# First token group: down projection of nine pairs in seven products of eight, and the sums of w_down made there

## The chip, the cores and the metric

The kernel runs on one core of one Trainium2 chip. Its engines, by the names that the profile gives them, are PE (TensorE; PEld is its weight load), DVE (VectorE), ACT (ScalarE), POOL (GpSimd) and SP (SyncE, which here only issues transfers). The metric is the device time of one execution in microseconds; the runs shown are compared by their median. The profile is of one further execution, whose times are counted from its first instruction.

## The reference

One layer of a hybrid decoder is computed for 2048 prompt tokens and 8 single decode tokens, 2056 columns in all, in float32. What the change touches is the feed-forward part behind the mixing of tokens:

```python
hn = _rmsnorm(h, norm2_g)
ff = jax.nn.silu(jnp.einsum('btd,df->btf', hn, w_gate)) * jnp.einsum('btd,df->btf', hn, w_up)
y = h + jnp.einsum('btf,fd->btd', ff, w_down)
```

The model width is 1024 and the width of `ff` 2816. A last normalisation of `y` gives the output.

## The kernel before

Values are transposed: features lie on the 128 partitions, tokens along the row. A float32 operand is held as a high part (a cast to fp32r, made by ACT) and a low part (value minus high part, a subtraction on DVE or POOL), and a product is three matmuls: high by high, high by low, low by high.

The program has two phases. The first (norm, input projection, recurrence, attention, output projection) takes the first 679 us. The second is the feed-forward part. It runs over three token groups (`HALVES`), each of two halves of 344 or 342 tokens. Within a group it runs over 11 pairs of 128-wide chunks of `ff` (`NPAIR`). In each pair the gate and the up projection are 2 × 2 block products done in seven products instead of eight (Strassen-Winograd; `PRODS` is their order), 12 matmuls each. Their weight blocks are partly sums of blocks: group 0 makes these on POOL (`mixed_weights`, L1259), splits all seven blocks of gate and up (L1224 and L1225, engines by `E_LO0`) and stores four of them split; groups 1 and 2 load those four and split only the other three (`E_LO1`, `E_LO2`).

`products` then makes the activations: ACT and DVE bring the results out of PSUM (L1410, L1431 to L1438), silu is on ACT (L1389), the multiply on POOL or DVE (L1392). The helper `part` casts a block on ACT (L1380) and subtracts on DVE (L1381).

The down projection has two forms, chosen by `wino(gi, p)`:

- plain: `down_weights` loads and splits four blocks of w_down per pair (POOL does all four subtractions), and `down` does 96 matmuls into 16 PSUM tiles `pd`, each followed by one add into `y` on DVE (L1469).
- in seven products: `down_make` loads quarters of w_down, forms eight half-wide sums (L1326, engines by `E_DSUM`), splits them in seven tiles `wd` (`split_parts`, L1293 and L1294) and stores five tiles of sums to `sums_d`; `down_load` reads the stored ones instead of forming them. `products` makes three more blocks of activations from four differences (L1399 to L1406, engines by `E_T1`, `E_T2`) and splits seven blocks instead of four. `down_parts` does 84 matmuls in 14 rounds, with 28 adds into `y` on DVE (L1500). Its rounds are spread between the products of the next pair.

Pairs 0 and 10 always use the plain form. Pairs 1 to 9 use the second form in groups 1 and 2, and the plain one in group 0. Group 1 runs `down_make`, group 2 `down_load`.

The order on each engine is fixed when the program is built. Each piece of work is a generator that yields the time for which it is planned; `plan()` lays these out from `wino` and a few constants (`U_M` for a product, `U_D` for a plain down projection, `U_R` for a round), and a scheduler turns the priorities into one list per engine. `PE_ORDER` writes the order on PE out by hand up to pair 1 of group 0. Weights go through 7 raw tiles and 8 split tiles in turn, sums of weights through 5 tiles (`sqp`, `bcp`), and larger blocks through 16 tiles of `bigp`.

Of the kernel before, what the change touches and what calls it, by code (L numbers as in the profile page):

```python
# [10 lines left out]
ALU = mybir.AluOpType  # L11
AX = mybir.AxisListType

P = 128
# [22 lines left out]
NPAIR = NF // 2  # L37
# [27 lines left out]
E_LO0 = ['V', 'V', 'V', 'V', 'P', 'P', 'P']  # L65
E_LO1 = ['P', 'V', 'P']
E_LO2 = ['V', 'V', 'P']
E_DLO1 = ['P', 'P', 'P', 'V', 'P', 'V', 'V']
E_DLO2 = ['V', 'P', 'V', 'P', 'V', 'V', 'P']
E_DSUM = ['P', 'P', 'P', 'P', 'P', 'P', 'P', 'V']  # L70
E_T1 = ['P', 'P', 'P', 'P']
E_T2 = ['P', 'V', 'P', 'P']
E_HN = ['P', 'V', 'P', 'P']
# [1 line left out]


def wino(gi, p):
    return gi > 0 and 0 < p < NPAIR - 1


def plan():
# [23 lines left out]
T_B, T_END, T_PROD, T_DOWN, T_ROUND = plan()  # L105
# [182 lines left out]
def hybrid_step(tc, xT, xR, vecs, cst, gatew, win, wout, wgate, wup, wdown, kT, vC, ck, cv, sconv, sh0,  # L288
                yT, pkT, pvT, pconv, phs, skw, svw, sconv_o, sh_o):
    nc = tc.nc  # L290
    ch = Chains(tc)
    at, ahead, fire = ch.at, ch.ahead, ch.fire
    with ExitStack() as ctx:
# [179 lines left out]
        def eng(x):  # L473
            return nc.gpsimd if x == "P" else nc.vector
# [703 lines left out]
        with ExitStack() as bctx:  # L1178
# [32 lines left out]
            def t_prod(gi, p, x, i):  # L1211
                return T_PROD[gi, p, x, i]
# [20 lines left out]
            def mixed_weights(src, gi, p, x):  # L1233
# [5 lines left out]
                if gi:  # L1239
                    for i, r in enumerate(PRODS):  # L1240
# [9 lines left out]
                        else:  # L1250
                            keep_weights((x, gi, p, r), f"{x}{gi}_{p}_{r}", v, eng((E_LO1, E_LO2)[gi - 1][(1, 2, 4).index(r)]))
                    return
# [38 lines left out]
            def split_parts(gi, p, j, v):  # L1291
                w = whl_tile(f"wd{gi}_{p}_{j}").rearrange("p a (b c) -> p a b c", b=2)
                nc.scalar.copy(w[:, :, 0], v)  # L1293
                eng((E_DLO1, E_DLO2)[gi - 1][j]).tensor_tensor(  # L1294
                    w[:, :, 1], v, w[:, :, 0].bitcast(F32), op=ALU.subtract)
                ws["d", gi, p, j] = w
                fire(("d", gi, p, j))
# [62 lines left out]
            def products(gi, p, x):  # L1360
                nn = HALVES[gi][0][1]
                name = f"{x}{gi}_{p}"
                up = x == "u"
                if up:
                    fh = {(h, n): fp.tile([P, TP], F32R, tag=f"fh{h}{n}", name=f"fh{gi}_{p}_{h}{n}")
                          for h in range(2) for n in range(2)}
                    fl = {(h, n): fp.tile([P, TP], F32R, tag=f"fl{h}{n}", name=f"fl{gi}_{p}_{h}{n}")
                          for h in range(2) for n in range(2)}
                C = {(h, n): (gpb if up else gpa).tile([P, TP], F32, tag="c", name=f"c_{name}_{h}{n}") for h in range(2) for n in range(2)}
                if not up:  # L1370
                    gss[gi, p] = C
                c11, c12, c21, c22 = (C[h, n][:, :nn] for h in range(2) for n in range(2))
                combine = up and wino(gi, p)
                if combine and gi not in extra:
                    place = slots(bigp, "big", f"t{gi}", F32R)
                    extra[gi] = [next(place) for _ in range(6)]

                def part(r, v, place):
                    hi, lo = (x[:, :nn] for x in place)
                    nc.scalar.copy(hi, v)  # L1380
                    nc.vector.tensor_tensor(lo, v, hi.bitcast(F32), ALU.subtract)  # L1381
                    ts[gi, p, r] = hi, lo
                    fire(("T", gi, p, r))

                def finished(h, n, src=None):
                    v = C[h, n][:, :nn]
                    src = v if src is None else src
                    if not up:
                        seen[f"act{gi}_{p}_{h}{n}"] = nc.scalar.activation(v, src, AF.Silu)  # L1389
                        return  # L1390
                    g = gss[gi, p][h, n][:, :nn]
                    (nc.vector if p == NPAIR - 1 or src is not v else eng(E_MUL[2 * h + n])).tensor_tensor(  # L1392
                        v, src, g, op=ALU.mult)
                    if not combine:
                        part((h, n), v, (fh[h, n], fl[h, n]))
                    elif (h, n) != (0, 1):
                        part({(0, 0): 1, (1, 0): 2, (1, 1): 3}[h, n], v, (fh[h, n], fl[h, n]))
                    if combine and (h, n) == (0, 1):
                        eng((E_T1, E_T2)[gi - 1][0]).tensor_tensor(c11, c12, c11, op=ALU.subtract)  # L1399
                        part(5, c11, (fh[0, 1], fl[0, 1]))  # L1400
                    elif combine and (h, n) == (1, 0):
                        eng((E_T1, E_T2)[gi - 1][1]).tensor_tensor(c12, c22, c12, op=ALU.subtract)
                        eng((E_T1, E_T2)[gi - 1][2]).tensor_tensor(c22, c22, c11, op=ALU.subtract)
                        part(6, c22, extra[gi][0:2])
                        part(7, c12, extra[gi][2:4])
                        eng((E_T1, E_T2)[gi - 1][3]).tensor_tensor(c21, c21, c22, op=ALU.subtract)  # L1406
                        part(4, c21, extra[gi][4:6])

                def add(o, a, b, op=ALU.add):
                    nc.vector.tensor_tensor(o, a, b, op)  # L1410

                banks = {}
                for i, r in enumerate(PRODS):
                    yield t_prod(gi, p, x, i), (x, gi, p, r), ("hn", gi, r)
                    key = BANK[r]
                    fresh = key not in banks
                    if fresh:
                        banks[key] = acc_tile(f"ps_{name}_{r}")[:, :nn]
                    ps = banks[key]
                    w = ws.pop((x, gi, p, r))  # L1420
                    for kk in range(4):
                        hi, lo = hn[gi, r, kk]
                        hi, lo = hi[:, :nn], lo[:, :nn]
                        wh, wl = w[:, 0, kk * P:kk * P + P], w[:, 1, kk * P:kk * P + P]
                        first = fresh and kk == 0
                        mm(f"{name}_{r}", ps, wh, hi, start=first, stop=False, skip_group_check=not fresh)
                        mm(f"{name}_{r}", ps, wh, lo, start=False, stop=False, skip_group_check=not fresh)
                        mm(f"{name}_{r}", ps, wl, hi, start=False, stop=kk == 3, skip_group_check=not fresh)
                    with ahead(F_LEAD[5]):
                        if r == 1:  # L1430
                            nc.scalar.copy(c21, ps)  # L1431
                        elif r == 2:
                            add(c11, c21, ps)
                            finished(0, 0)
                        elif r == 6:
                            seen[f"c{name}_6"] = nc.scalar.copy(c12, ps)  # L1436
                        elif r == 5:
                            nc.scalar.copy(c22, ps)  # L1438
                        elif r == 7:
                            add(c22, c22, ps)  # L1440
                            finished(1, 1)
                        elif r == 3:
                            add(c12, c12, ps)
                            finished(0, 1)
                        else:
                            finished(1, 0, ps)
                fire((x + "done", gi, p))
# [152 lines left out]
            for gi in range(len(HALVES)):  # L1600
                tb = T_B[gi]
                if gi:
                    ch.add(hn_mix(gi, stage, T_MIX[gi], F_MIX[2 * gi - 1]))
                    ch.add(hn_load(gi, PRODS[:3], slots(bigp, "big", f"hn{gi}_0", F32R), tb - F_HN[0], U_M))
                ch.add(hn_load(gi, PRODS[3:], slots(hnp, "hn", f"hn{gi}_1", F32R), tb - F_HN[1], U_M, None if gi else stage))
                ch.add(y_load(gi, tb + F_HN[2]))
                for i, n in enumerate((1, 0)):
                    te = T_END[gi]
                    ch.add(finish(gi, n, te + F_FIN[0] + F_FIN[1] * i, 1.0) if gi < 2 else finish_last(n))
                for p in range(NPAIR):  # L1610
                    ch.add(mixed_weights(wgate, gi, p, "g"))
                    ch.add(mixed_weights(wup, gi, p, "u"))
                    ch.add((down_load if gi == 2 else down_make)(gi, p) if wino(gi, p) else down_weights(gi, p, T_DOWN[gi, p]))
                    ch.add(products(gi, p, "g"))
                    ch.add(products(gi, p, "u"))
                    ch.add((down_parts if wino(gi, p) else down)(gi, p))
# [113 lines left out]
```

## Time and profile before

| what | value |
|---|---|
| three runs | 2061.11 to 2063.26 us, median 2062.06 us |
| span of the profiled execution | 2054.6 us (the time from its first to its last instruction; its own device time is not given beside it, the median is 7.5 us above the span) |
| granted TensorE clock, mean | 0.997 |
| group 0, 720 to 1105 us | PE busy 385.00 of 385 us |
| group 1, 1181 to 1563 us | PE busy 376.44 of 382 us |
| group 2, 1640 to 2000 us | PE busy 360.00 of 360 us |

Busy time of an engine is the time in which one of its instructions was running. Stretches are given by their start and end in us from the first instruction. A group of instructions is told by the line of the kernel, the engine, the operation and the tiles that it writes and reads; a tile has the name that the code gives it (`pw` and `pd` are PSUM tiles of the down projection, `wd` and `w_d` its split weights, `sd` its sums, `fl` and `t` low parts of activations).

### The profile page before, as it was taken

What the parts mean: (1) busy time and instruction counts of PE and PEld (TensorE: products, weight loads), DVE (VectorE), ACT (ScalarE), POOL (GpSimd) and SP (SyncE); (2) the same over time, 40 slices, a digit from 0 to 9 for tenths busy, and PEclk for the clock granted to TensorE, in tenths of its full rate; (3) what the DMA queues carried; (4) which work ended last, traced back from release to release, by engine and by line L of the source; (5) the groups of instructions that cost most, each with busy time, mean ns of one, the idle gap of its engine ahead of it and who ended that gap; (6) DMA issues with size and microseconds to landing.
All of it is one profiled execution on the core that took longest, in us unless ns stands there. A gap on an engine that the chain in (4) does not pass through costs nothing.

```text
span 2054.6 us, 34857 instructions
## 1 busy us (share of the span) xinstructions
PE 2015.9 (98%) x12319; PEld 1908.1 (93%) x12319; DVE 1459.9 (71%) x2694; ACT 944.6 (46%) x1960; POOL 906.5 (44%) x799
## 2 busy tenths in 40 slices
PE   9999999999999999999999999999999999999998
PEld 9988787878777899999999999999999999999998
DVE  6877886767985766666654667777768666777675
ACT  6764774553664543343334533333335433433343
POOL 5311342020122787567656645556457522322333
PEclk9999999999999999999999999999999999999999
DMA  9864584576688856666546677776677675566652
GB/s 329 293 213 143 188 275 159 175 233 210 208 261 280 314 200 223 205 210 207 207 172 210 229 260 258 227 229 221 222 253 265 211 251 189 183 197 196 197 179 96
DMA packets 208991, 450.98 MB, mean 219 GB/s; under 512 B 25232, under 2 KB 82720, under 8 KB 208800
## 3 DMA queue, kind: packets, MB, share of 16 engines
q1 hardware_dynamic: 205184, 445.73, 65.2%
q10 hardware_dynamic: 3632, 3.02, 0.4%
q8 instruction: 97, 1.59, 0.3%
q14 instruction: 78, 0.64, 0.1%
HBM read 335.89 MB, written 113.84 MB: 219 GB/s over the span
## 4 chain that ended last, share of the span: by engine, by line
PE 77%; DVE 9%; DMA 6%; ACT 3%; issue 2%; POOL 1%; SPq 0%; DVEq 0%; ACTq 0%; POOLq 0%
PE ps_u L396 19%; PE ps_g L396 19%; PE pw L396 11%; PE pd L396 10%; PE ip L396 10%; PE op L396 4%; DMA n<-hs 3%; DMA xs<-in_xT 1%; DMA m<-mixed 1%; PE o L396 1%; PE pt L401 1%; DVE sc L974 1%; DVE sc L963 1%; PE s L396 1%; DMA mixed<-n 1%
## 5 line engine op out<-in xcount | busy, mean ns | idle before, releaser
L396 PE MATMUL ps_g<-hn,w_g 128*128 128x342 f32 (+1 forms) x2772 | 489.4, 320 | 4.6 <-DVE c_u L1410 1.8
L396 PE MATMUL ps_u<-hn,w_u 128*128 128x342 f32 (+1 forms) x2772 | 479.9, 319 | 1.9 <-ACT c_u L1436 1.3
L396 PEld LDWEIGHTS ps_g<-hn,w_g 128*128 128x128 f32 x2772 | 445.1, 188 | 6.0 <-DVE c_u L1410 2.3
L396 PEld LDWEIGHTS ps_u<-hn,w_u 128*128 128x128 f32 x2772 | 444.2, 188 | 2.6 <-ACT c_u L1436 1.6
L396 PE MATMUL ip<-xn,w_in 128*128 128x512 f32 (+1 forms) x1680 | 353.4, 358 | 1.9 <-ACT xn L431 1.8
L396 PEld LDWEIGHTS ip<-xn,w_in 128*128 128x128 f32 x1680 | 270.1, 189 | 46.0 <-issue 3.8
L1500 DVE TENSOR_TENSOR y<-y,pw 128x342 f32<-128x342 f32 x504 | 238.7, 504 | 73.0 <-PE pw L396 72.2
L396 PE MATMUL pd<-fh,w_d 128*128 128x344 f32 (+1 forms) x960 | 239.4, 320 | 0.6 <-DVE y L1469 0.6
L396 PE MATMUL op<-mix,w_out 128*128 128x512 f32 (+1 forms) x960 | 203.4, 357 | 0.5 <-DVE rrec L763 0.3
L396 PEld LDWEIGHTS op<-mix,w_out 128*128 128x128 f32 x960 | 155.4, 188 | 29.3 <-issue 5.0
L1469 DVE TENSOR_TENSOR y<-y,pd 128x344 f32<-128x344 f32 (+1 forms) x240 | 117.9, 507 | 75.3 <-PE pd L396 70.7
L396 PEld LDWEIGHTS pd<-fh,w_d 128*128 128x128 f32 x960 | 168.3, 188 | 1.4 <-DVE y L1469 1.1
L396 PE MATMUL pw<-fh,wd 128*128 128x342 f32 x576 | 165.6, 319 | 1.2 <-DVE y L1500 1.2
L396 PE MATMUL pd<-fl,w_d 128*128 128x344 f32 (+1 forms) x480 | 153.4, 320 | 0.0
L1381 DVE TENSOR_TENSOR fl<-c_u,fh 128x342 fp32r<-128x342 f32 (+1 forms) x132 | 107.1, 815 | 48.3 <-ACT fh L1380 47.9
L1225 POOL TENSOR_TENSOR w_u<-ru,w_u 128x512 fp32r<-128x512 f32 x44 | 58.9, 1338 | 181.6 <-ACT w_u L1224 155.0
L1392 POOL TENSOR_TENSOR c_u<-c_u,c_g 128x342 f32<-128x342 f32 (+1 forms) x60 | 60.5, 1008 | 170.7 <-DVE c_u L1410 132.1
L1380 ACT CAST fh<-c_u 128x342 fp32r<-128x342 f32 (+1 forms) x132 | 63.0, 480 | 157.8 <-POOL c_u L1392 61.9
L396 PE MATMUL pw<-t,wd 128*128 128x342 f32 x648 | 126.7, 320 | 2.6 <-DVE t L1381 1.7
L1410 DVE TENSOR_TENSOR c_u<-c_u,ps_u 128x342 f32<-128x342 f32 (+1 forms) x99 | 50.2, 507 | 100.3 <-PE ps_u L396 100.1
L396 PEld LDWEIGHTS pw<-t,wd 128*128 128x128 f32 x648 | 106.0, 188 | 4.4 <-DVE t L1381 2.5
L396 PEld LDWEIGHTS pw<-fh,wd 128*128 128x128 f32 x576 | 105.3, 189 | 1.7 <-DVE y L1500 1.5
(316 smaller groups left out, 3507.4 us busy)
## 6 DMA issues: line engine op xcount, KB each, us to landing
w_g<-split_g SPq DMA_DIRECT2D x88, 512.0 KB, 4.2
w_u<-split_u SPq DMA_DIRECT2D x88, 512.0 KB, 4.9
w_in<-split_w SPq DMA_DIRECT2D x84, 512.0 KB, 3.5
rg<-in_wgate SPq DMA_DIRECT2D x110, 256.0 KB, 3.1
ru<-in_wup SPq DMA_DIRECT2D x110, 256.0 KB, 3.2
w_out<-split_w SPq DMA_DIRECT2D x48, 512.0 KB, 4.4
split_g<-w_g SPq DMA_DIRECT2D x44, 512.0 KB, 3.6
split_u<-w_u SPq DMA_DIRECT2D x44, 512.0 KB, 2.7
```

The source lines that it names most:

```text
L396: r = nc.tensor.matmul(*args, **kw)
L401: r = nc.tensor.transpose(*args)
L963: seen[f"sm{gb}_{kv}_{g}"] = nc.vector.tensor_tensor_reduce(sc[:, g, :kn], ps[:, gi * 256:gi * 256 + kn], mask[:, k0:k0 + kn], -SCALE, ns[ ...
L974: nc.vector.tensor_scalar(sc[:, g, :kn], sc[:, g, :kn], mx[:, 1, g:g + 1], None, ALU.mult)
L1225: lo_eng.tensor_tensor(w[:, 1, :], src, w[:, 0, :].bitcast(F32), op=ALU.subtract)
L1380: nc.scalar.copy(hi, v)
L1381: nc.vector.tensor_tensor(lo, v, hi.bitcast(F32), ALU.subtract)
L1392: (nc.vector if p == NPAIR - 1 or src is not v else eng(E_MUL[2 * h + n])).tensor_tensor(v, src, g, op=ALU.mult)
L1410: nc.vector.tensor_tensor(o, a, b, op)
L1469: r = nc.vector.tensor_tensor(ys[gi, n, m], ys[gi, n, m], ps, ALU.add)
L1500: nc.vector.tensor_tensor(v, v, ps, ALU.add)
```

## The change

`wino` no longer leaves group 0 out, so that pairs 1 to 9 of group 0 take the form in seven products; two lists name the engines of its new subtractions and differences. Group 0 now runs `down_make`, and groups 1 and 2 run `down_load`. `plan()` follows from `wino` by itself; no other constant changes.

```diff
+E_DLO0 = ['P', 'V', 'P', 'V', 'P', 'V', 'V']
...
+E_T0 = ['P', 'P', 'P', 'P']
...
 def wino(gi, p):
-    return gi > 0 and 0 < p < NPAIR - 1
+    return 0 < p < NPAIR - 1
...
-                eng((E_DLO1, E_DLO2)[gi - 1][j]).tensor_tensor(
+                eng((E_DLO0, E_DLO1, E_DLO2)[gi][j]).tensor_tensor(
                     w[:, :, 1], v, w[:, :, 0].bitcast(F32), op=ALU.subtract)
...
-                        eng((E_T1, E_T2)[gi - 1][0]).tensor_tensor(c11, c12, c11, op=ALU.subtract)
+                        eng((E_T0, E_T1, E_T2)[gi][0]).tensor_tensor(c11, c12, c11, op=ALU.subtract)
...
-                    ch.add((down_load if gi == 2 else down_make)(gi, p) if wino(gi, p) else down_weights(gi, p, T_DOWN[gi, p]))
+                    ch.add((down_load if gi else down_make)(gi, p) if wino(gi, p) else down_weights(gi, p, T_DOWN[gi, p]))
```

The three other differences of `products` (L1402, L1403, L1406) get their engine from `E_T0` in the same way. 'P' is POOL and 'V' is DVE.

More of the change, by code (lines that the diff above doesn't have):

```diff
@@ L1398, in finished @@
                     if combine and (h, n) == (0, 1):
-                        eng((E_T1, E_T2)[gi - 1][0]).tensor_tensor(c11, c12, c11, op=ALU.subtract)
+                        eng((E_T0, E_T1, E_T2)[gi][0]).tensor_tensor(c11, c12, c11, op=ALU.subtract)
                         part(5, c11, (fh[0, 1], fl[0, 1]))
                     elif combine and (h, n) == (1, 0):
-                        eng((E_T1, E_T2)[gi - 1][1]).tensor_tensor(c12, c22, c12, op=ALU.subtract)
-                        eng((E_T1, E_T2)[gi - 1][2]).tensor_tensor(c22, c22, c11, op=ALU.subtract)
+                        eng((E_T0, E_T1, E_T2)[gi][1]).tensor_tensor(c12, c22, c12, op=ALU.subtract)
+                        eng((E_T0, E_T1, E_T2)[gi][2]).tensor_tensor(c22, c22, c11, op=ALU.subtract)
                         part(6, c22, extra[gi][0:2])
                         part(7, c12, extra[gi][2:4])
-                        eng((E_T1, E_T2)[gi - 1][3]).tensor_tensor(c21, c21, c22, op=ALU.subtract)
+                        eng((E_T0, E_T1, E_T2)[gi][3]).tensor_tensor(c21, c21, c22, op=ALU.subtract)
                         part(4, c21, extra[gi][4:6])
```

## The prediction

> **What bounds the kernel now.** I read the head of the page first, then the busy time by stretch, then single engines inside one stretch of each token group.
>
> ```profile
> span 2054.6 us, 34857 instructions
> PE 2015.9 (98%) x12319; PEld 1908.1 (93%) x12319; DVE 1459.9 (71%) x2694; ACT 944.6 (46%) x1960; POOL 906.5 (44%) x799
> ```
>
> The median of the runs is 2062.06 us, so 7.5 us lie outside the span; I add changes of the span to the median. PE is the bound as an average. The table by stretch (length, then busy time of PE, PEld, DVE, ACT, POOL) asks whether that holds in each group: rows one to three are the middles of groups 0, 1 and 2, the fourth is the passage from group 1 to group 2, the fifth the fullest DVE stretch that I found.
>
> ```profile
> 720.00:1105.00 385.00, 385.00 (x2451) 385.00 (x2450) 245.79 (x368) 152.73 (x303) 258.97 (x194) 1.00 0.59 202
> 1181.00:1563.00 382.00, 376.44 (x2384) 373.45 (x2383) 281.83 (x496) 136.59 (x277) 210.15 (x191) 1.00 0.71 235
> 1640.00:2000.00 360.00, 360.00 (x2295) 360.00 (x2294) 254.77 (x473) 134.36 (x271) 104.60 (x89) 1.00 0.63 200
> 1582.00:1622.00 40.00, 39.43 (x248) 38.63 (x247) 28.02 (x43) 20.50 (x49) 27.11 (x26) 1.00 0.76 265
> 1542.00:1582.00 40.00, 40.00 (x256) 40.00 (x255) 33.33 (x57) 21.08 (x47) 25.09 (x23) 1.00 0.75 248
> ```
>
> Group 0, which the change touches, never starves PE: 385.00 of 385. Group 1, which already does what group 0 is now to do, loses 382 − 376.44 = 5.6 us; group 2, which loads the sums instead of making them, loses none. The granted clock is 1.00 in all of them. So group 0 gains exactly as long as PE stays the bound there, and the question is what DVE and POOL have left.
>
> **What PE saves.** The price of a matmul comes from back-to-back work in the order of time:
>
> ```profile
> 740.05 7.24 PE L396 MATMUL ps_u<-hn,w_u 128*128 128x344 f32 x45
> 747.14 2.06 PE L396 MATMUL ps_g<-hn,w_g 128*128 128x344 f32 x12
> ```
>
> (747.14 − 740.05) / 45 = 0.1576 us. A pair of group 0 is 14 products of 12 matmuls and 96 for the down projection: 264, or 41.6 us. Seven products of eight need 84: 252, or 39.7 us. Nine pairs save 108 matmuls, **17.0 us**, if nothing stalls.
>
> **What DVE and POOL pay.** These are groups by line and shape, group 0 (720 to 1098 us) for what goes, group 1 (1222 to 1542 us) for what comes; busy us and mean ns stand behind the bar.
>
> ```profile
> L1469 DVE TENSOR_TENSOR y<-y,pd 128x344 f32<-128x344 f32 x145 | 72.1, 508 | 50.9 <-PE pd L396 50.6
> L1381 DVE TENSOR_TENSOR fl<-c_u,fh 128x344 fp32r<-128x344 f32 x36 | 26.5, 737 | 15.5 <-ACT fh L1380 15.5
> L1225 POOL TENSOR_TENSOR w_d<-rd,w_d 128x512 fp32r<-128x512 f32 x36 | 52.6, 1467 | 5.9 <-ACT w_d L1224 5.9
> L1500 DVE TENSOR_TENSOR y<-y,pw 128x342 f32<-128x342 f32 x222 | 103.4, 504 | 19.4 <-PE pw L396 19.1
> L1381 DVE TENSOR_TENSOR fl<-c_u,fh 128x342 fp32r<-128x342 f32 x30 | 28.1, 941 | 6.2 <-ACT fh L1380 5.9
> L1381 DVE TENSOR_TENSOR t<-c_u,t 128x342 fp32r<-128x342 f32 x24 | 21.1, 899 | 0.0
> L1294 DVE TENSOR_TENSOR wd<-rd,wd 128x512 fp32r<-128x512 f32 x16 | 16.0, 1003 | 0.0
> L1326 DVE TENSOR_TENSOR sd<-rd,rd 128x256 f32<-128x256 f32 x8 | 6.1, 767 | 7.3 <-DMA rd<-in_wdown 7.3
> L1294 POOL TENSOR_TENSOR wd<-rd,wd 128x512 fp32r<-128x512 f32 x16 | 22.3, 1395 | 16.4 <-ACT wd L1293 14.7 <-DVE c_u L1392 1.7
> L1326 POOL TENSOR_TENSOR sd<-rd,sd 128x256 f32<-128x256 f32 x15 | 14.8, 984 | 0.6
> L1326 POOL TENSOR_TENSOR rd<-rd 128x256 f32<-128x256 f32 x8 | 6.7, 831 | 2.2 <-DMA rd<-in_wdown 2.2
> L1406 POOL TENSOR_TENSOR c_u<-c_u,c_u 128x342 f32<-128x342 f32 x8 | 8.8, 1100 | 1.9 <-DVE fl L1381 1.5
> L1399 POOL TENSOR_TENSOR c_u<-c_u,c_u 128x342 f32<-128x342 f32 x7 | 6.5, 931 | 10.0 <-DVE c_u L1392 10.0
> ```
>
> DVE, for one pair: 28 adds into y instead of 16, 28 × 0.466 − 16 × 0.497 = +5.1; seven low parts of the activations instead of four, 7 × 0.911 − 4 × 0.736 = +3.4; four of the seven low parts of the down weights (E_DLO0), 4 × 1.00 = +4.0; one sum, +0.8. Together +13.3. Now DVE has 245.79 us in 385 / 41.6 = 9.25 pairs, 26.6 each. After the change it needs **39.9 us in a pair that PE would do in 39.7**.
>
> POOL, for one pair: the four w_d subtractions go, −4 × 1.46 = −5.8; three wd come, 3 × 1.39 = +4.2; seven sums between 0.83 and 0.98, +6.4; the four differences of E_T0 between 0.93 and 1.10, +4.1. Together +8.9 on 258.97 / 9.25 = 28.0: **36.9 of 39.7**.
>
> Both cannot be that full and keep these durations, for they get in each other's way. Over the whole trace (minimum/median/maximum ns):
>
> ```profile
> L1500 DVE TENSOR_TENSOR y<-y,pw x504: 494/503/515, 1220.6 to 2017.6; 128x342 f32<-128x342 f32 x168
> L1381 DVE TENSOR_TENSOR fl<-c_u,fh x132: 500/793/1658, 706.1 to 2026.1; 128x342 fp32r<-128x342 f32 x88, 128x344 fp32r<-128x344 f32 x44
> L1225 DVE TENSOR_TENSOR w_u<-ru,w_u x55: 675/687/1821, 685.1 to 2000.1; 128x512 fp32r<-128x512 f32 x55
> ```
>
> The add that reads PSUM always takes 0.50 us. The subtraction of the same width that reads SBUF alone takes 0.50 at best and 1.66 at worst. The order of time in group 1 shows why:
>
> ```profile
> 1351.07 1.57 POOL L1294 TENSOR_TENSOR wd<-sd,wd 128x512 fp32r<-128x512 f32 x1
> 1351.83 1.18 DVE L1381 TENSOR_TENSOR t<-c_u,t 128x342 fp32r<-128x342 f32 x1
> 1352.60 1.56 POOL L1225 TENSOR_TENSOR w_u<-ru,w_u 128x512 fp32r<-128x512 f32 x1
> 1353.78 0.94 DVE L1294 TENSOR_TENSOR wd<-sd,wd 128x512 fp32r<-128x512 f32 x1
> ```
>
> The first POOL row ends at 1352.64 and DVE's t at 1353.01, 0.37 later; the second ends at 1354.16 and DVE's wd at 1354.72, 0.56 later. DVE began in the middle of a POOL instruction and got its result only behind it. The Trainium skill (SBUF — State Buffer, Who interferes with whom) says that a DVE instruction with two SBUF inputs and a GpSimd one that reads SBUF exclude each other for a whole instruction. These rows agree; were they to run side by side, the sum would be rival one's.
>
> So I bound DVE's need from both sides. Without waits, SBUF subtractions would take 0.50 (342 wide) and 0.68 (512 wide). Of the 39.9 us, the seven activation parts then save 7 × 0.41 = 2.9 and the four wd 4 × 0.32 = 1.3. Three more rows of group 0 give the rest:
>
> ```profile
> L1225 DVE TENSOR_TENSOR w_u<-s_u,w_u 128x512 fp32r<-128x512 f32 x18 | 18.7, 1038 | 1.5 <-ACT w_u L1224 1.0 <-DMA rd<-in_wdown 0.3
> L1392 DVE TENSOR_TENSOR c_u<-c_u,c_g 128x344 f32<-128x344 f32 x9 | 13.9, 1545 | 0.0
> L529 DVE TENSOR_TENSOR n<-n,n 128x342 f32<-128x342 f32 x16 | 16.5, 1030 | 0.2
> ```
>
> Eight gate and up low parts save 8 × 0.36 = 2.9, the one multiply 1.0, and the mixing for group 1 (sixteen of these over nine pairs, and as many of L521) about 1.1. That leaves 30.7. At the other end every one of some 24 such instructions waits a full 1.0 us as L1392 does (1.545 less 0.50): 30.7 + 24 = 55. Between them I take the waits that DVE has, 9.2, scaled by POOL's share, from 258.97 / 385 = 67% to 36.9 / 39.7 = 93%: 12.8, or **43.5 us** with DVE never idle. The lower value is the nearer, because POOL is then idle 7% of the time and DVE's PSUM adds run beside it: I take 42.8, against 41.6 now.
>
> Nine pairs: 9 × (42.8 − 41.6) = +11 us. DVE cannot be always busy; the mixing for group 1 waits for transfers. In group 0 that is the first row, and behind such a wait stand adds that free PSUM banks, so PE waits in turn, as rows two and three (PEld, group 1) show it already:
>
> ```profile
> DVE n L521 <- DMA n<-hs: 11.8, 8, 3.3
> PEld pw L396 <- DVE y L1500: 3.2, 4, 1.5
> PEld pw L396 <- DVE t L1381: 2.5, 3, 1.4
> ```
>
> Up to 11.8 us come on top, less what the weights made ahead absorb; I take +3. Group 0: **+14 us**.
>
> Group 1 loads now. Seven sums on POOL and one on DVE go from each pair, and it comes near to group 2, which stalls for nothing: −5.6 at most, I take **−4**.
>
> At nothing:
>
> ```profile
> L1380 ACT CAST t<-c_u 128x342 fp32r<-128x342 f32 x54 | 25.5, 476 | 14.7 <-POOL c_u L1402 5.5 <-POOL c_u L1403 3.9 <-POOL c_u L1406 3.4
> L1293 ACT CAST wd<-rd 128x512 fp32r<-128x512 f32 x99 | 61.4, 620 | 76.1 <-PE ps_u L396 25.2 <-issue 21.7 <-PE pw L396 20.1
> ```
>
> ACT gets three more casts of 0.476 and three of 0.620 per pair, 3.3 us on 152.73 / 9.25 = 16.5, hidden in a 40 us pair. DMA: group 0 stores five sums of 256 KB and reads ten quarters of 128 KB instead of four of 256, 1.5 MB more in 40 us, 38 GB/s on 202; group 1 runs at 235. SP issues ten loads, not four, and five stores per pair; in group 1 a store waits behind its sum and loads stand behind it:
>
> ```profile
> SPq L1343 <- POOL sd L1326: 12.4, 12, 3.1
> ```
>
> That is 1 us a time, against sums that the code asks for 9 us ahead (L_DS); if POOL lags it joins the stall. The two tiles for t0 take the last of 16 big buffers, so the first loads of group 1's hn wait for group 0's; the passage from group 1 to 2 has that state and costs 40 − 39.43 = 0.6 us. I count 0.
>
> Sum: 2062.06 + 14 − 4 = **2072**; its own range 2066 to 2084.
>
> **Rivals.** *PE keeps its pace* (faster). If DVE's waits vanish into gaps, 30.7 to 39.7 us fit, and the time is 2062 − 17 − 0 to 5.6: 2039 to 2045, with a few stalls to 2057. For it: PE held 40.00 of 40 with DVE at 33.33. Against: no stretch shows DVE above 83%, and here it needs 39.9 with today's waits. The point is a DVE pair of 39.7. The Trainium skill (Perfetto Trace Analysis, Identifying the Most-Contended Engine) would start from the engine with most occupancy, PE here, and by that its 17 us are the gain. Chance 0.25.
>
> *It cancels*: DVE at 41.0 to 41.9 per pair, −5 to +3, less group 1's: within 0.2%. Chance 0.17.
>
> *Both engines jam*: DVE and POOL wait on each other and on PE, DVE is busy only 93% of its time, 42.8 / 0.93 = 46.0: 9 × 4.4 − 4 = +36, 2084 to 2098. For it: the sums share five sq and bc buffers with eight gate and up sums per pair. Chance 0.13.
>
> **Chances.** Forecast 0.45, rivals 0.25, 0.17, 0.13. A difference of 0.2% (4.1 us) is about what a measurement of this kernel can tell. Slower 0.45 + 0.13 = 0.58, same 0.17, faster 0.25. The range leaves out the best of rival one and the worst of three: 2043 to 2092.
>
> **What would show it.** Right: in group 0 PE loses its full 385 of 385, its waits name DVE (y, t, c_u) or weights' low parts, DVE stands at 95% or more and POOL above 85%; L1381 and L1225 on DVE have longer means; the pair takes over 41.6 us. In group 1 PE's idle time falls from 5.6 us towards 0. Wrong: PE full in group 0 at 39.7 us a pair with DVE under 90%; or stalls that name DMA or ACT.

## The result, and the profile after

The changed kernel takes 2096.73 us (median of 4 runs, 2095.84 to 2101.4), the one before 2062.66. The ratio is 1.0169, 95% interval 1.0155 to 1.0184: 34 us slower. Lines of the code lie two further down from here on (L1381 is now L1383, L1500 is L1502, and so on).

The head of the page of the changed kernel, and then its busy time by stretch, with the stretches of before (length; busy time of PE, PEld, DVE, ACT, POOL; granted clock; DMA share; GB/s):

```profile
span 2095.5 us, 35036 instructions
PE 2024.4 (97%) x12211; PEld 1902.7 (91%) x12211; DVE 1556.1 (74%) x2865; ACT 967.2 (46%) x2014; POOL 940.8 (45%) x826
```

```profile
720.00:1105.00 385.00, 354.87 (x2132) 344.00 (x2131) 313.51 (x482) 156.55 (x317) 309.80 (x251) 0.97 0.61 211
1181.00:1563.00 382.00, 379.76 (x2423) 378.02 (x2422) 264.49 (x481) 146.71 (x304) 168.57 (x144) 1.00 0.68 224
1640.00:2000.00 360.00, 359.55 (x2294) 358.91 (x2293) 248.30 (x460) 136.73 (x278) 109.80 (x95) 1.00 0.62 199
```

PE executes 108 matmuls fewer (12319 − 12211), as worked out, and is busy longer. Group 1 is cured: its idle time falls from 5.6 to 2.2 us. The loss lies in group 0: PE is idle for 30.1 of 385 us and its clock is 0.97. Yet DVE is busy for only 81% of the stretch (313.51 / 385) and POOL for 80%. No engine is full.

The starts of pair 1's and of pair 10's gate product on PE bound the nine pairs that the change touches. These are the first kernel's rows, then the changed one's:

```profile
707.47 1.26 PE L396 MATMUL ps_g<-hn,w_g 128*128 128x344 f32 x7
...
1080.38 1.27 PE L396 MATMUL ps_g<-hn,w_g 128*128 128x344 f32 x7
```

```profile
711.07 1.26 PE L398 MATMUL ps_g<-hn,w_g 128*128 128x344 f32 x7
...
1122.42 0.48 PE L398 MATMUL ps_g<-hn,w_g 128*128 128x344 f32 x2
```

**372.9 us became 411.3**, 45.7 a pair. The busy time in these two stretches, before and after:

```profile
707.47:1080.38 372.91, 372.91 (x2374) 372.91 (x2373) 239.57 (x357) 148.10 (x294) 255.00 (x190) 1.00 0.59 203
711.07:1122.42 411.35, 379.86 (x2288) 368.42 (x2286) 330.93 (x510) 167.64 (x340) 331.58 (x269) 0.97 0.61 210
```

They hold 2288 matmuls instead of 2374, 86 fewer and not 108: pair 0's plain down projection lies inside, and a part of pair 9's rounds behind. At the pace of before, 372.91 / 2374 = 0.157 us each, PE would need 359 us for them. So 52 us are lost against that pace, 38 against before. The same stretch is the yardstick for all experiments. From the starts of the groups' first gate products, group 1 takes 449.5 us instead of 454.1.

One caution on the kernel before. In each run of the changed kernel the device time is 1.75 to 1.84 us above the span, so the 7.5 us that the prediction puts outside the span are not there: the profiled execution of the kernel before was some 6 us faster than its median. The two spans differ by 41 us, the medians by 34, and every comparison with 372.9 carries this.

Next, what the engines waited for in 720 to 1105 us (total, times, longest). First the longest waits before:

```profile
ACT w_u L1224 <- PE pd L396: 83.5, 24, 7.1
DVE y L1469 <- PE pd L396: 52.0, 76, 3.6
POOL w_u L1225 <- ACT w_u L1224: 47.3, 18, 5.9
```

and after, the longest, with the largest of PEld further down in the list:

```profile
ACT fh L1382 <- POOL c_u L1394: 37.3, 13, 6.7
ACT wd L1295 <- POOL sd L1328: 34.5, 12, 6.0
DVE fl L1383 <- ACT fh L1382: 25.0, 17, 4.5
ACT c_g L1391 <- DVE c_g L1412: 24.5, 13, 4.4
POOL s_g L1261 <- DMA rg<-in_wgate: 18.7, 5, 5.5
POOL sd L1328 <- DMA rd<-in_wdown: 18.5, 11, 2.9
...
PEld pw L398 <- DVE y L1502: 13.7, 9, 4.2
```

Read the direction. Before, ACT, which begins the splitting of the weights, waited 83.5 us for PE: weights were made as fast as PE gave tiles back, ahead of need. After, ACT waits for POOL, POOL for loads and DVE for ACT: I read this as a chain that supplies PE with little lead left, though each engine in it has idle time.

### The profile page after: what moved, and what is told of

Its sections match the earlier page's. It is cut to its first block, busy times and chain, and to the rows that moved or that the text cites. A ratio compares the mean times of both kernels' runs of the same rounds, so it can differ in the third digit from the quotient of the medians.

```text
span 2095.5 us, 35036 instructions
## 1 busy us (share of the span) xinstructions
PE 2024.4 (97%) x12211; PEld 1902.7 (91%) x12211; DVE 1556.1 (74%) x2865; ACT 967.2 (46%) x2014; POOL 940.8 (45%) x826
## 3 DMA queue, kind: packets, MB, share of 16 engines
q8 instruction: 96, 1.57, 0.3%
## 5 line engine op out<-in xcount | busy, mean ns | idle before, releaser
L398 PE MATMUL ps_g<-hn,w_g 128*128 128x342 f32 (+1 forms) x2772 | 501.0, 322 | 12.4 <-DVE c_u L1412 4.7
L398 PE MATMUL ps_u<-hn,w_u 128*128 128x342 f32 (+1 forms) x2772 | 496.6, 320 | 8.4 <-ACT c_u L1438 5.1
L1502 DVE TENSOR_TENSOR y<-y,pw 128x342 f32<-128x342 f32 (+1 forms) x756 | 358.2, 503 | 87.8 <-PE pw L398 86.0
L398 PE MATMUL pw<-fh,wd 128*128 128x342 f32 (+1 forms) x864 | 254.2, 324 | 10.7 <-DVE y L1502 9.0
L398 PE MATMUL pw<-t,wd 128*128 128x342 f32 (+1 forms) x972 | 194.8, 323 | 8.1 <-DVE y L1502 5.3
L398 PEld LDWEIGHTS pw<-t,wd 128*128 128x128 f32 x972 | 160.7, 190 | 13.3 <-DVE y L1502 6.8
L398 PEld LDWEIGHTS pw<-fh,wd 128*128 128x128 f32 x864 | 160.0, 191 | 13.9 <-DVE y L1502 11.3
L1383 DVE TENSOR_TENSOR fl<-c_u,fh 128x342 fp32r<-128x342 f32 (+1 forms) x132 | 115.5, 883 | 60.4 <-ACT fh L1382 59.6
L1295 ACT CAST wd<-rd 128x512 fp32r<-128x512 f32 x162 | 100.5, 620 | 120.3 <-PE ps_u L398 46.1
L1296 POOL TENSOR_TENSOR wd<-rd,wd 128x512 fp32r<-128x512 f32 x81 | 111.6, 1379 | 98.6 <-ACT wd L1295 92.5
L398 PE MATMUL pw<-fl,wd 128*128 128x342 f32 (+1 forms) x432 | 139.8, 324 | 2.6 <-DVE fl L1383 2.6
L398 PE MATMUL pd<-fh,w_d 128*128 128x342 f32 (+1 forms) x384 | 95.7, 321 | 0.6 <-DVE y L1471 0.6
```

Of the source, the lines that this page charges most:

```text
L398: r = nc.tensor.matmul(*args, **kw)
L1296: eng((E_DLO0, E_DLO1, E_DLO2)[gi][j]).tensor_tensor(w[:, :, 1], v, w[:, :, 0].bitcast(F32), op=ALU.subtract)
L1502: nc.vector.tensor_tensor(v, v, ps, ALU.add)
```

## The experiments

Each experiment edits the changed kernel, and its line numbers move by a few. The letters in the expectations (one that is not in this list is told where it stands): A, DVE is full (the prediction); B, the multiply comes late from POOL; C, the stores of sums; D, the use of SBUF that DVE and POOL share, whichever does the work; E, a sum that waits for its load holds up POOL's queue; H, loads, the raw tiles they hold and SP's single queue delay other weights; W, the work in DVE's and POOL's queues. "Nine pairs" is the stretch defined above, in one profiled execution. The runs of one kernel differ by 5.6 us in the changed one and by up to 12.4 (e19; 11.1 in e17), and the rounds left over at the stretch's end make some 25 matmuls, 4 us, of difference, so I read nothing into a few us of it.

| label | median us | ratio to before, 95% | nine pairs us |
|---|---|---|---|
| before | 2062.66 | 1 | 372.9 |
| after | 2096.73 | 1.0169 [1.0155, 1.0184] | 411.3 |
| e1_no_store | 2114.48 | 1.0259 [1.0244, 1.0274] | 408.2 |
| e2_no_sums | 2089.75 | 1.0138 [1.0119, 1.0158] | 403.6 |
| e3_mul_dve | 2102.25 | 1.0203 [1.0185, 1.0221] | 405.9 |
| e4_lo_act | 2082.14 | 1.0098 [1.0082, 1.0114] | 399.7 |
| e6_wd_act | 2090.98 | 1.0134 [1.0109, 1.0159] | 397.5 |
| e7_lo_dve_act | 2075.83 | 1.0064 [1.0045, 1.0084] | 390.7 |
| e8_pairs_6_to_9 | 2088.23 | 1.0118 [1.0102, 1.0135] | 380.7 |
| e9_pairs_1_4_7 | 2080.73 | 1.0089 [1.0068, 1.011] | 386.3 |
| e10_sums_of_ones | 2094.63 | 1.0155 [1.0138, 1.0172] | 399.9 |
| e11_loads_early | 2103.0 | 1.0202 [1.0186, 1.0217] | 410.4 |
| e12_ones_and_lo | 2070.99 | 1.0045 [1.0027, 1.0063] | 386.9 |
| e13_sums_late | 2094.82 | 1.0161 [1.0143, 1.018] | 411.1 |
| e14_no_lo | 2058.38 | 0.9977 [0.9965, 0.9988] | 374.0 |
| e15_no_lo_pool | 2073.48 | 1.0063 [1.0045, 1.0081] | 389.2 |
| e16_no_lo_dve | 2078.78 | 1.0082 [1.0067, 1.0097] | 389.6 |
| e17_sums_only | 2088.03 | 1.0124 [1.0101, 1.0147] | 404.3 |
| e19_no_loads | 2110.08 | 1.0233 [1.0198, 1.0268] | 390.3 |
| e20_sums_no_loads | 2087.56 | 1.0118 [1.01, 1.0137] | 377.4 |

**Stores and the multiply.** e1_no_store takes the stores out of group 0, so that group 1 makes and stores the sums again:

```diff
-                    if j not in (3, 6):
+                    if gi and j not in (3, 6):
-                    ch.add((down_load if gi else down_make)(gi, p) if wino(gi, p) ...
+                    ch.add((down_load if gi == 2 else down_make)(gi, p) if wino(gi, p) ...
```

> The first group makes its sums but does not store them; the second group makes and stores them as before the change. Theory A (VectorE is full, with its waits for GpSimd) and theory B (the multiply of the activations comes late out of GpSimd's queue, and the cast, the low part and all adds behind it on VectorE come late with it): group 0 changes by less than 5 us, group 1 gets back its 4.6 us of stalls, 2095 to 2105 us. Theory C (GpSimd waits for loads, because SyncE's queue stands behind the new stores): group 0 loses at least 15 us of its stalls, 2075 to 2087 us.

Group 0 stays (485.8 us as a whole against 486.2), and group 1 loses its gain and more (467.5 against 449.5). C falls. e3_mul_dve puts group 0's multiplies on DVE (`or not gi` in the condition that picks DVE):

> In group 0 the two multiplies per pair that GpSimd does go to VectorE, directly behind the add that feeds them. Theory A: VectorE has 1.0 to 1.8 us more per pair, 2106 to 2113 us. Theory B: VectorE no longer waits for GpSimd's queue in the middle of its own, 2070 to 2087 us. Theory C: no change beyond 4 us.

The nine pairs gain 5 us at most and the total gets 5.5 us worse. The wait above, `ACT fh <- POOL c_u` with 37.3 us, comes back as a wait for DVE:

```profile
ACT fh L1382 <- DVE c_u L1394: 35.9, 18, 4.7
```

So the multiply is as late from DVE's queue, and B, which blames POOL's, falls. What a multiply in time would be worth, this run does not show.

**Work taken off DVE or POOL.** In group 0, e2_no_sums replaces the eight sums of a pair by copies on ACT, e4_lo_act the six gate and up low parts that POOL makes, e7_lo_dve_act the eight that DVE makes, e6_wd_act the four of w_down on DVE:

```diff
-                    eng(E_DSUM[...]).tensor_tensor(S[r], a, b, op=op)
+                    nc.scalar.copy(S[r], b)
...
+                if lo_eng is nc.gpsimd and not key[1] and key[0] != "d":
+                    nc.scalar.copy(w[:, 1, :], src)
+                else:
```

> Leaves out the eight sums of w_down per pair: ScalarE copies one block in their place, so loads, stores and tiles stay. GpSimd has 6.5 us less per pair, VectorE 0.7 us less. Theory A: VectorE's gain is 0.7 us and some 2 us of waits per pair, 25 us in nine pairs, about 2072 us. Theory B: GpSimd's queue is short enough that the multiply is in time, most stalls and the half-clock stretches go, 2050 to 2065 us. Theory C: the loads are as late as before, 2085 to 2097 us.

> Leaves out six low parts of the gate and up weights per pair of group 0: ScalarE copies the block there in place of GpSimd's subtraction. GpSimd has 8.7 us less per pair, ScalarE 3.7 us more. Theory A: VectorE waits less for GpSimd, 2 to 3 us per pair, 2070 to 2080 us. Theory B: 2045 to 2065 us. Theory C: the loads stay late, 2080 to 2097 us.

> Leaves out the eight low parts of the gate and up weights per pair of group 0 that VectorE makes: ScalarE copies the block there. It is the counterpart of the run that took six such low parts from GpSimd. VectorE has 8.7 us less per pair. Theory A: group 0 comes to within 1.5 us of PE's 39.7 us per pair, 2040 to 2052 us, and the half-clock stretches go. Theory D: it gives little more than the GpSimd run, 2070 to 2085 us.

> Leaves out the four low parts of the down weights per pair that VectorE makes in group 0 (E_DLO0): ScalarE copies the block there. VectorE has 4.8 us less per pair. Theory A (VectorE's queue is the bound: its work of 38 us per pair and some 8 us in which the head of its queue waits): nine pairs lose 4 to 5 us each, 2053 to 2062 us. Theory D (the two engines' shared use of SBUF is the bound, whichever of them the work is on): the same use taken from GpSimd in the fourth run gave 15 us, here four instead of six such instructions that are shorter, so less than 10 us, 2087 to 2097 us.

Theory A expected 2053 to 2062 us from e6 and 2040 to 2052 from e7; they took 2091.0 and 2075.8. In the nine pairs, work taken from DVE gives 21 us (e7) and 14 (e6; its profiled execution was 5.5 us faster than its median), work taken from POOL 12 (e4). So work in either queue counts, and A as a matter of DVE's throughput alone falls. Both totals lie in D's ranges, but D can't be the whole: e10 and e19 below keep this work and gain in the stage. e2 gives 8 us only; its copies, in ACT's queue, wait for the same loads.

**Does the loss add up over pairs?** `wino` limited to pairs 6 to 9, and to 1, 4 and 7, of group 0:

```diff
-    return 0 < p < NPAIR - 1
+    return (0 if gi else 5) < p < NPAIR - 1
...
+    return 0 < p < NPAIR - 1 and (gi > 0 or p % 3 == 1)
...
```

> Correct version: in group 0 only pairs 6 to 9 go in seven products; the second group loads the sums of those four pairs and makes the others. Theory A: 4/9 of the loss of group 0 and 4/9 of the gain of group 1, about 2077 us; if the mixing for group 1, which is over by about pair 6, is what fills VectorE, the four pairs keep PE's pace: 2062 - 4 x 1.9 - 2 = about 2053 us.

> Correct version: in group 0 only pairs 1, 4 and 7 go in seven products; the second group loads the sums of those three and makes the others. Theory A as a matter of totals: VectorE has two plain pairs with 15 us of slack each between two full ones, so it catches up, the stalls are small and the time is 2062 - 3 x 1.9 - 1.5 = 2055, up to 2062 us with 2 us of stalls per pair. If the loss comes with each such pair by itself (from the order of its own chain), 3/9 of it stays: about 2074 us.

Both took longer than either theory expected (2088.2 and 2080.7 us). Here the nine pairs hide a part, since pair 9's rounds lie behind them. From group 0's first gate product to group 1's, 443.0 us before, three such pairs far apart (e9, 459.6) cost 16.6 us, four in a row (e8, 465.0) 22.0 and nine (486.2) 43.2: 5.5, 5.5 and 4.8 each. So the loss comes with each pair, and a full queue that builds up over many pairs is not needed. In e9 one such stall can be followed in the order of time; most of DVE's, PEld's and some other rows are left out:

```profile
877.98 2.14 SPq L527 DMA_DIRECT2D mixed<-n  x3
...
880.21 0.38 SPq L1307 DMA_DIRECT2D rd<-in_wdown  x1
880.69 0.41 SPq L1238 DMA_DIRECT2D ru<-in_wup  x1
880.90 0.50 DVE L1412 TENSOR_TENSOR c_u<-c_u,ps_u 128x344 f32<-128x344 f32 x1
881.19 0.86 SPq L1307 DMA_DIRECT2D rd<-in_wdown  x2
...
883.47 0.73 POOL L1328 TENSOR_TENSOR sd<-rd,sd 128x256 f32<-128x256 f32 x1 [4.92 <-DMA rd<-in_wdown]
884.16 0.93 POOL L1394 TENSOR_TENSOR c_u<-c_u,c_g 128x344 f32<-128x344 f32 x1
...
885.12 0.48 ACT L1382 CAST fh<-c_u 128x344 fp32r<-128x344 f32 x1 [4.92 <-POOL c_u L1394]
885.51 0.44 ACT L1438 COPY c_u<-ps_u 128x344 f32<-128x344 f32 x1
...
886.00 1.21 PE L398 MATMUL ps_u<-hn,w_u 128*128 128x344 f32 x6 [0.86 <-ACT c_u L1438]
```

SP issues the loads of w_down behind three stores of the mixing. POOL is idle 4.92 us for them, in front of a sum; behind the sum stands a multiply, whose input DVE had ready at 881.40 and which starts at 884.16; behind the multiply's cast on ACT stands the copy that empties a PSUM bank, and PE waits for that. The wait that the list shows for PE, 0.86 us for ACT, lies three queues (ACT, POOL, SP) away from its cause.

**The loads in the changed kernel.** e10_sums_of_ones lets the sums of group 0 read a resident tile (loads stay), e11_loads_early asks for the quarters 5 us earlier, e13_sums_late plans sums and splits 3 us later, e12_ones_and_lo joins e10 and e7:

```diff
+                    a, b = (a, b) if gi else (mask, mask)
...
-                        yield t - (L_RW if j else L_DR)
+                        yield t - (L_RW if j else L_DR) - (0 if gi else 5)
...
-                    yield t - L_DS
+                    yield t - L_DS + (0 if gi else 3)
```

> Leaves out the operands of the w_down sums of group 0: they are formed from a resident tile of ones, with the same instructions, loads and stores, so that GpSimd no longer waits for the loads there. Theory E (head of line: SyncE's stores hold up the loads, GpSimd stands at a sum that waits for its load, the multiply behind it is late, then ScalarE's cast with the copies out of PSUM behind it, then VectorE's low part with the adds behind it): GpSimd's 21 us of waits for these loads go and the stalls with them, 2070 to 2083 us. Theory A or D (work of the two engines, and their shared use of SBUF): no work goes, 2090 to 2099 us.

> Correct version: in group 0 the quarters of w_down are asked for 5 us earlier, so their loads have 10 us instead of 5 before the sums. Theory E: if the buffers let them start, most of the 21 us of waits go, 2075 to 2088 us. Theory A or D: 2093 to 2101 us.

> Both at once: the sums of group 0 are formed from ones, and the eight low parts of the gate and up weights that VectorE makes are copied by ScalarE instead. If A and E are two causes side by side, their gains add: 2076 less another 15 to 20 us, 2052 to 2062 us. If E is what was left after VectorE's work went, nothing else is, 2040 to 2050 us. If E is not a cause, 2070 to 2078 us.

> Correct version: in group 0 the sums and the split of the down weights are planned 3 us later, behind the same loads, so they stand behind other work of GpSimd instead of in front of it. Theory E: 2080 to 2092 us, with the waits of GpSimd for loads of w_down under 10 us; if the weights are then too late for PE, waits of pw for wd appear and the time is above 2097 us. Theory A or D: 2093 to 2101 us.

By the totals E falls: e10 gains 2 us. By stages it doesn't: the nine pairs gain 11 us, and the total hides it, because group 0 begins 6 us later (at 685.9 us, 679.8 in the changed kernel) and group 1 takes 3 us more. Why it begins later stays open: e12 fills the same tile of ones and begins at 678.6. Such an edit is to be read from its stage. Moving the loads or the sums in time (e11, e13) gains nothing in the stage, and early loads make the total 6 us worse: these two shifts found no slack. e12 gains 24 us in the nine pairs where e10 and e7 alone gain 11 and 21, and 33.1 us over group 0 as a whole where they gain 13.5 and 22.8. So the two gains nearly add up; how far they overlap lies within the play of the yardstick.

**All low parts of gate and up.** e14_no_lo leaves them out in group 0 (the third matmul reads the high part instead), e15 only POOL's six, e16 only DVE's eight:

```diff
+                bare = not key[1] and key[0] != "d" and True
+                if bare:
+                    high_only.add(key)
+                else:
+                    lo_eng.tensor_tensor(w[:, 1, :], src, w[:, 0, :].bitcast(F32), op=ALU.subtract)
...
+                        b = 0 if (x, gi, p, r) in high_only else 1
+                        wh, wl = w[:, 0, kk * P:kk * P + P], w[:, b, kk * P:kk * P + P]
```

> Leaves out all 14 low parts of the gate and up weights per pair of group 0, on VectorE and GpSimd; the third matmul reads the high part again, ScalarE gets nothing more, PE's work and the bytes stored stay. If the work in the two queues together is the cause: PE keeps within 1 us of 39.7 us per pair, 2040 to 2050 us. If it is the order of the rounds in group 0, stalls of 2 to 3 us per pair stay, 2062 to 2075 us.

> Leaves out only the six of these low parts that GpSimd makes. The run in which ScalarE copied in their place had 2082 us. If ScalarE's 3.7 us more per pair took nothing back: 2079 to 2085 us. If ScalarE's queue is one of the three that count: 2065 to 2076 us.

> Leaves out only the eight low parts that VectorE makes. With ScalarE's copies in their place it was 2076 us. If ScalarE's 5 us more per pair took nothing back: 2073 to 2079 us. If ScalarE's queue counts: 2052 to 2068 us. Theory A (VectorE alone is the bound) would have 2040 to 2050 us.

Nine pairs: −22 (POOL's), −22 (DVE's), −37 (both). Six instructions on POOL are worth as much as eight on DVE. ACT's six copies in e4 took back 10.5 us of POOL's 22 (399.7 against 389.2), its eight in e7 nothing (390.7 against 389.6); why they differ is not shown. The stretch of e14:

```profile
720.00:1105.00 385.00, 375.00 (x2348) 369.98 (x2347) 256.98 (x465) 173.48 (x352) 247.80 (x224) 1.00 0.69 234
```

With DVE at 67% and POOL at 64%, less than POOL had before (258.97), PE still loses 10 us, and the nine pairs are 16 us above PE's pace. Something other than the engines' work is left.

**The sums alone, and without their loads.** e17_sums_only gives group 0 its plain down projection back and lets it make and store the sums beside it, with ten more loads per pair. e20_sums_no_loads is e17 without these loads; sums and stores are of ones. e19_no_loads takes the ten loads per pair out of the changed kernel in the same way.

```diff
 e17
-    return 0 < p < NPAIR - 1
+    return gi > 0 and 0 < p < NPAIR - 1
+                    if not gi and 0 < p < NPAIR - 1:
...
+                        ch.add(down_make(0, p, False))
 e20 (and e19 with "if gi")
-                    for i in {0: (0, 7, 2), 3: (3,), 4: (8, 6)}.get(j, ()):
+                    for i in {0: (0, 7, 2), 3: (3,), 4: (8, 6)}.get(j, ()) if split else ():
...
-                            nc.sync.dma_start(sums_d[p, j], pre[j])
+                            nc.sync.dma_start(sums_d[p, j], pre[j] if split else mask.unsqueeze(1).to_broadcast([P, 2, 256]))
```

> Correct version: group 0 keeps the plain down projection, but makes and stores the sums beside it, and the second group loads them. GpSimd has 6.4 us more per pair (34 of 41.6), VectorE 0.8 us more. If work in the queues only stalls where both are filled: group 0 stalls under 3 us, group 1 keeps its gain of 4.6 us, 2056 to 2062 us. If the sums and their transfers by themselves hold up group 0: 2066 to 2080 us.

> Group 0 of the changed kernel asks for no quarter of w_down in pairs 1 to 9 (ten loads and four raw tiles per pair go, two raw tiles that are now held only for the length of a sum stay); sums are made, splits cast and subtracted and five tiles stored as before, but all from a resident tile of ones, so DVE, POOL and ACT issue the same instructions. Theory H (the loads, the raw tiles that they hold and SP's single queue delay the other weights, and that is most of the loss): 2055 to 2072 us, a pair of group 0 near 42 us or less, POOL's waits for rg and ru loads fewer. Theory W (the loss is in the work and the order of DVE's and POOL's queues, whatever is loaded): within 5 us of the 2094.6 that the sums of ones gave, so 2088 to 2098. Between them: both count, and the difference to 2094.6 is the share of the loads and their tiles.

> The kernel in which group 0 keeps its plain down projection and only makes and stores the sums (2088 us), without the ten loads per pair for the sums: sums of ones, stores of ones. POOL and DVE make as many sums. Theory H: 2055 to 2065 us, about the kernel before less group 1's 4.6 us, plus little. Theory W: POOL's seven sums per pair (6.4 us on 28.0 of 41.6) delay what stands behind them: 2080 or more.

In e19 and e20 the total misleads again. Group 0 begins at 707.1 us (e20) and 708.8 (e19) instead of 678.9. A store of ones waits for no sum, and all 45 of them moved into the passage before group 0. The first and the last of them in e20 (the tile of ones has the name `cs`; in e19 they lie between 621 and 670 us):

```profile
619.34 4.08 SPq L1349 DMA_DIRECT2D sums_d<-cs  x5
...
663.76 4.32 SPq L1349 DMA_DIRECT2D sums_d<-cs  x6
```

So in group 0 these kernels are without the stores as well as without the loads. The times expected for them can't be read from the totals, so I take the stretch from 740 us on, about where pair 1 starts in the later two. e17, with its longest wait on POOL there, and e20:

```profile
740.00:1105.00 365.00, 343.64 (x2124) 339.02 (x2123) 213.65 (x331) 132.02 (x264) 267.24 (x220) 0.98 0.71 241
```

```profile
POOL sd L1328 <- DMA rd<-in_wdown: 30.2, 10, 7.8
```

```profile
740.00:1105.00 365.00, 362.29 (x2295) 360.39 (x2295) 233.98 (x354) 143.17 (x286) 291.58 (x246) 1.00 0.58 202
```

This is the clearest pair of the study. e20's POOL is fuller (291.58 us against 267.24), and e20's PE is idle for 2.7 us where e17's is for 21.4. What e20 lacks in the stage are transfers: ten loads and five stores per pair, and the raw tiles held for them (four go, two more are held for a shorter time). The nine pairs say the same: making sums costs 4.5 us (377.4 − 372.9, no more than runs of one kernel differ by), their transfers 26.9 more (404.3 − 377.4). What the stores have of this is open. Leaving them out of the changed kernel gave 3 us (e1, 411.3 − 408.2), but in e17 SP waits in 720 to 1105 us for stores to set raw tiles free:

```profile
SPq L1238 <- DMA sums_d<-rd: 11.9, 5, 5.2
```

e20's longest wait in 720 to 1105 us is that of before again, with ACT ahead of PE:

```profile
ACT w_u L1229 <- PE pd L398: 76.0, 21, 7.9
```

It is no sure sign of a lead, for e17 has it too (740 to 1105 us), and e17 starves PE:

```profile
ACT w_u L1226 <- PE pd L398: 66.9, 15, 11.7
```

In the changed kernel the transfers are worth 21.0 us (411.3 − 390.3). Sums that do not wait for their loads gain 11.4 of them (e10); the rest lies in tiles, places in SP's queue and stores, which no run parts. e19 is still 35 us above PE's pace, with DVE and POOL busier than in the changed kernel (87% and 86%):

```profile
740.00:1105.00 365.00, 344.76 (x2113) 333.88 (x2112) 317.74 (x472) 157.35 (x315) 313.31 (x254) 0.99 0.49 171
```

So W and H, with the stores added to it, are both right for a part. Of the 52 us above PE's pace, 37 go without the low parts and 21 without the transfers; together 58, the whole and a little more. The two were not left out in one kernel, so how far they overlap is not shown. Nor do the runs part the loads from the stores, or SP's queue from the raw tiles. No version that computes everything beats the kernel before; e14, which leaves a part out, is 0.23% faster.

## Why the prediction was wrong

It said slower, at 2072.0 us with 2092 as the upper end; it came out at 2096.7. Its steps in turn:

- **PE saves 108 matmuls**: right by count, and it needs a supply that keeps up. Group 0 never had it.
- **DVE's need and POOL's need**: POOL's was right. 309.80 us in 385 / 45.7 = 8.42 pairs is 36.8 a pair, 36.9 was forecast. DVE needed 313.51 / 8.42 = 37.2, and 307.04 / 8 = 38.4 over pairs 2 to 9, without pair 0's plain adds; not 39.9, nor 42.8 with longer waits:

```profile
750.73:1122.42 371.69, 340.20 (x2036) 328.76 (x2034) 307.04 (x476) 153.09 (x311) 299.77 (x243) 0.97 0.62 213
```

  These rows of DVE in the changed kernel (720 to 1105 us) show what was right in it and what was not:

```profile
L1502 DVE TENSOR_TENSOR y<-y,pw 128x344 f32<-128x344 f32 x205 | 96.6, 501 | 5.2 <-PE pw L398 4.7
L1383 DVE TENSOR_TENSOR fl<-c_u,fh 128x344 fp32r<-128x344 f32 x33 | 31.9, 976 | 25.1 <-ACT fh L1382 25.0
L1383 DVE TENSOR_TENSOR t<-c_u,t 128x344 fp32r<-128x344 f32 x24 | 20.2, 841 | 3.0 <-ACT t L1382 2.9
L523 DVE SCALAR_TENSOR_TENSOR n<-n,vec,hb 128x342 f32<-128x342 f32 x16 | 14.7, 920 | 15.4 <-DMA n<-hs 15.4
L1227 DVE TENSOR_TENSOR w_u<-s_u,w_u 128x512 fp32r<-128x512 f32 x16 | 12.9, 818 | 0.4 <-ACT w_u L1226 0.4
L1394 DVE TENSOR_TENSOR c_u<-c_u,c_g 128x344 f32<-128x344 f32 x8 | 6.9, 863 | 0.1
```

  The add that reads PSUM stays at 0.50 us, and the subtraction in SBUF goes from 737 to 976 ns, which fits the exclusion of DVE and POOL. Other rows in SBUF got shorter, though: `w_u<-s_u` from 1038 to 818 ns, the multiply from 1545 to 863. In all DVE's waits did not grow with POOL's share: 38.4 less the 30.7 without waits is 7.7 us a pair; 9.2 was counted with the durations of before, and 12.8 was forecast.
- **From need to time, "43.5 us with DVE never idle"**: this is the step that failed. DVE was idle for 19% of the stretch. A pair took 45.7 us, not 42.8, though DVE needed less than was thought. Work on DVE and POOL did delay PE (37 us by e14), but as delay along a chain that passes from SP to POOL, ACT, DVE and PE and back through the tiles (followed at one stall of e9; that the other stalls are like it is argued from the waits). A need per pair compared with PE's 39.7 can't see that.
- **"At nothing: SP issues ten loads, not four, and five stores"**: the second failure, and the larger in kind. The prediction named it ("if POOL lags it joins the stall") and counted 0. These transfers and their tiles are worth 21 us in the changed kernel (e19) and 27 beside the plain down projection (e20). Group 1 before the change ran with the same transfers for 5.6 us of idle time, but there three weights of seven are split, not seven, and no gate and up sums are made: that this left it a lead to spend is argued, not shown.
- **Idle time of the mixing, +3 us**: 15.4 us of waits for `n` against 11.8 before, 3.6 more; how much of that reached PE is not shown.
- **Group 1, −4 us**: right, −4.6 (454.1 to 449.5). e1 takes it away again.
- **The jam, 46.0 us per pair, 2084 to 2098**: its numbers came, 45.7 us and 2096.7; its mechanism, both engines waiting on each other while DVE is busy 93% of its time, did not: 81%. So the number came by luck. The range ended below its upper part.
- **What would show it**: DVE at 95% and POOL above 85% did not come; most of the longer means, over 41.6 us a pair, and waits that name `y` and `c_u` did. The named waits were no proof of the cause: `PEld pw <- DVE y` stands at the end of the chain. A sign of being wrong came too: `PEld ps_u <- ACT c_u`, 6.0 us in the same list.

## What to carry to other kernels

A group that runs without a stall has a lead: engines that make its inputs wait for PE. One long wait of this kind does not prove it (e17). Before adding work there, ask for each stream (loads, tiles, each in-order queue) what stands behind the new instruction when its input is late; busy shares of 80% don't tell. And read an experiment from the stage that it edits: three here moved the start of the stage by 6 to 29 us, and their totals pointed the wrong way. Ask also what else an edit sets free: without their operands, the stores left the stage with the loads.

## What the runs showed of the hardware that was not expected

Gaps that together fill about half of 3.4 us on PE halve its clock. The changed kernel, three successive stretches of 3.40 us in group 0 and PE's rows at the turn:

```profile
948.90:952.30 3.40, 1.57 (x9) 0.99 (x7) 3.40 (x7) 1.38 (x3) 3.04 (x3) 1.00 0.85 335
952.30:955.70 3.40, 3.33 (x12) 3.33 (x13) 3.40 (x6) 2.16 (x6) 2.00 (x2) 0.50 0.46 131
955.70:959.10 3.40, 3.40 (x23) 3.40 (x23) 3.15 (x8) 0.39 (x1) 0.50 (x2) 1.00 0.23 77
```

```profile
950.13 1.21 PE L398 MATMUL ps_g<-hn,w_g 128*128 128x344 f32 x6 [0.88 <-DVE c_u L1394]
952.37 0.66 PE L398 MATMUL pw<-fl,wd 128*128 128x344 f32 x1 [1.02 <-DVE fl L1383]
952.82 0.49 PE L398 MATMUL pw<-fh,wd 128*128 128x344 f32 x1
```

PE was busy for 1.57 of 3.40 us, and for the next stretch the granted clock is 0.50, 12 matmuls instead of 23, and a single one takes 0.49 us where 0.32 is usual. The Trainium skill (TensorE: Matmul & The Clock Gate, What's actually happening) says that the clock is halved after an idle window of about 3.4 us. The length agrees; that the window must be idle does not, for no gap at this place is longer than 1.02 us. In 720 to 1105 us the clock falls at five more places; in the 3.40 us before them PE was busy for 0.01, 1.64, 1.28, 1.28 and 1.25 us. The least busy 3.40 us there, on the same grid, that kept the full clock had 1.91:

```profile
1037.60:1041.00 3.40, 1.25 (x8) 0.96 (x7) 3.40 (x4) 0.62 (x1) 2.64 (x2) 1.00 1.05 381
1041.00:1044.40 3.40, 3.32 (x11) 3.32 (x12) 2.90 (x7) 1.26 (x4) 2.36 (x3) 0.51 0.95 346
750.90:754.30 3.40, 1.91 (x13) 1.62 (x11) 2.36 (x2) 2.66 (x6) 2.50 (x2) 1.00 0.88 302
```

In this execution the border thus lies between 1.64 and 1.91 us of 3.40. The mean clock of 0.97 over 385 us puts the cost at some 12 us at most, (1 − 0.97) × 385, part of the 52: a stall costs more than its length. Before, that stretch ran at 1.00.
